# Odd mixer of a two-layer block: depthwise-convolution taps shared out anew between two engines, and the layer norm's sums moved in TensorE's order

## The chip, the cores and the metric

One core of a Trainium2 chip runs the kernel. The metric is the device time of one execution in microseconds (us), in fp32 throughout. TensorE (PE) multiplies matrices into PSUM, VectorE (DVE) and ScalarE (ACT) work on SBUF and PSUM, GpSimd (POOL) on SBUF, and SyncE (SP) issues the transfers.

## The reference, cut to what matters

The input is 512 tokens of 1024 channels. It goes through a first block, then a second block of two layers. The last layer is the odd mixer, and the change lies in it alone:

```python
def odd_mixer(h, w_in, dw_w, dw_b, ln_g, ln_b, w_out):
    proj = h @ w_in                                   # 1024 -> 3 x 1024
    a, b, gate = jnp.split(proj, [CONV_WIDTH, 2 * CONV_WIDTH], axis=-1)
    glu = a * jax.nn.sigmoid(b)
    conv = lax.conv_general_dilated(                  # causal, depthwise, 31 taps
        glu, dw_w.astype(glu.dtype), window_strides=(1,), padding=[(CONV_K - 1, 0)],
        dimension_numbers=('NWC', 'WIO', 'NWC'), feature_group_count=CONV_WIDTH)
    cf = conv.astype(jnp.float32) + dw_b.astype(jnp.float32)
    mu = jnp.mean(cf, axis=-1, keepdims=True)         # over the 1024 channels
    var = jnp.mean(jnp.square(cf - mu), axis=-1, keepdims=True)
    cn = (cf - mu) * lax.rsqrt(var + EPS) * ln_g.astype(jnp.float32) + ln_b.astype(jnp.float32)
    y = jax.nn.silu(cn).astype(h.dtype) * jax.nn.silu(gate)
    return y @ w_out
```

## The kernel before, in words

Channels lie on partitions, tokens along the free axis, so the mixer's 1024 channels are eight tiles (m = 0 to 7) of 128 x 512. A large product is made of "units": one unit gives one tile of 128 output channels as 24 matmuls, since each fp32 operand is split into a high and a low part and three products are summed (`mm3`, L302 to L304). The 512 KB of weights for each unit come by one transfer from SP (`prefetch`, L270) into one of three raw buffers, and ScalarE and GpSimd split them. Units have two PSUM banks in turn; a bank is free for the next unit but one when its result has been read.

The mixer's work is written out by hand as the string `P7_ORDER` (L69), and the loop at L1478 emits it step by step:

- a (`glu_tile`): two units, b and a, then the sigmoid on ScalarE and the product on VectorE. GpSimd also builds the small diagonal weights of the tile's taps (`wds`).
- t, u, v (`stack_tile`, L1360): TensorE regroups the product so that four shifts of 32 channels stand on 128 partitions.
- c (`conv_tile`): the 31 taps. A group of four taps is four matmuls of 32 output partitions side by side (L1376), each with two records in the trace; `PE_TAPS` says how many groups a tile has. Three taps (`N_POOL`) are scaled on ScalarE and added on GpSimd. The rest are VectorE's, one multiply-add each: two lead taps onto an SBUF tile (`P7_LEAD`), the others onto the PSUM bank into which TensorE summed its taps, the last from there into the tile `f`. They are not issued at once but kept in a list (`pend`) that is emitted while the next units are (`tick`), and emptied up to a tile by `drain`.
- s (`stats_tile`): the tile's parts are added up, less the mean of tile 0, and the running sum `msum` and the running sum of squares `ssum` are brought on; on GpSimd, but on VectorE for the last tile.
- g (`gate_tile`): one unit and a Silu on ScalarE out of its bank.
- x (`p8_residual`): four transposes of the residual for one block of tokens (L1471), evicted by ScalarE.
- l (`norm_stats`): TensorE sums `msum` and `ssum` over the channels by a matmul with ones (L405, one for each); VectorE makes mean and reciprocal root from them.
- b, n (`norm_tile`): the scale and shift are spread over the tile, then each tile is normalised, put through a Silu, multiplied by its gate and split into high and low parts for the output projection.

TensorE and SP run in the order in which the program emits (`manual_schedule`), VectorE too until l; from l on VectorE is ordered by the scheduler, as ScalarE and GpSimd are throughout. Each engine still runs its own queue in order. After the string comes the output projection: 8 tiles by 4 blocks of tokens, the first two blocks together, tile by tile, into four banks (two of them those of the units), then the third, then the fourth (`p8_last`).

Of the kernel before, what the change touches and what calls it, by code (L numbers as in the profile page):

```python
# [20 lines left out]
C = 128  # L21
# [39 lines left out]
N_FIRST = 6  # L61
N_POOL = (3, 3, 3, 3, 3, 3, 3, 3)
P7_LEAD = 2
PE_TAPS = (4, 4, 4, 4, 4, 4, 4, 4)
N_PE = max(PE_TAPS)
P7_ENG = {mybir.EngineType.PE, mybir.EngineType.SP}
P1_ENG = {mybir.EngineType.PE, mybir.EngineType.SP}
P7_ENG2 = {mybir.EngineType.DVE}
P7_ORDER = 'a0 a1 t0 g0 u0 a2 v1 c0 a3 v2 c1 s0 a4 v3 c2 s1 a5 v4 c3 s2 a6 v5 c4 s3 a7 v6 c5 s4 g1 v7 c6 s5 g2 c7 g3 s6 x0 g4 x1 s7 g5 x2 l0 g6 b0 n0 n1 n2 n3 n4 n5 g7 n6 n7 x3'  # L69
N_W = 10  # L70
RATE = 4.0
P7_LO = (1, 1)
# [80 lines left out]
def build(tc, xT, par, cst, rope, w_ab, w_in, w_rv, w_out, w_up, w_down, a_w, ab_w, c_w, co_w, post1, poolw, out, dbg=None):  # L153
# [8 lines left out]
    act, dve, pe, gps = nc.scalar, nc.vector, nc.tensor, nc.gpsimd  # L162

    def A(out, in_, func=AF.Copy, **k):
        return act.activation(out=out, in_=in_, func=func, **k)  # L165

    def TT(out, in0, in1, o, e=None):
        return (e or dve).tensor_tensor(out=out, in0=in0, in1=in1, op=o)  # L168

    def STT(out, in0, scalar, in1, o0, o1, e=None):  # L170
        return (e or dve).scalar_tensor_tensor(out=out, in0=in0, scalar=scalar, in1=in1, op0=o0, op1=o1)  # L171
# [5 lines left out]
    MUL, ADD, SUB, MAX = ALU.mult, ALU.add, ALU.subtract, ALU.max  # L177


    class Heap:  # L180
# [6 lines left out]
        def fr(self, *ts):  # L187
            self.free.extend(ts)

    def sbuf_heap(n, name, dt=F32, w=T):  # L190
        return Heap([hp.tile([128, w], dt, name=f"{name}{i}") for i in range(n)])

    al = sbuf_heap(N_ACT - 8, "act")
# [20 lines left out]
    fr = al.fr  # L214
# [8 lines left out]
    def cc(name, i=0, n=None):  # L223
        o, w = C_OFF[name]
        n = w if n is None else n
        o += i * n
        if o < C_KEEP:
            return ck[:, o:o + n]
        o -= C_KEEP
        assert o // T == (o + n - 1) // T  # L230
        return cs[o // T][:, o % T:o % T + n]

    def pc(name, i=0, n=1):
        o, _ = P_OFF[name]
        return pr[:, o + i * n:o + (i + 1) * n]
# [3 lines left out]
    def bc4(ap, n=NCH):  # L239
        return ap.unsqueeze(1).to_broadcast([ap.shape[0], n, ap.shape[1]])  # L240
# [40 lines left out]
    def take():  # L281
        return made.popleft()
# [31 lines left out]
    def tick(n=RATE):  # L314

        credit[0] += n
        while pend and credit[0] >= 1:
            credit[0] -= 1
            pend.popleft()[1]()
        if not pend:  # L320
            credit[0] = min(credit[0], 0)

    def drain(m):
        while pend and pend[0][0] <= m:
            credit[0] -= 1
            pend.popleft()[1]()
# [162 lines left out]
    n0 = P_OFF["attn_w"][1]  # L489
# [517 lines left out]
    acc = []  # L1007
    for t, p in enumerate(units(2 * KF, X, outer=4)):
# [5 lines left out]
        if gu:  # L1014
# [8 lines left out]
            acc = []  # L1023
# [15 lines left out]
    for (k0, kn) in SEGS:  # L1039
        for m in range(KD):  # L1040
            w = take()
# [40 lines left out]
    v2 = lambda t: t.rearrange("p (e n) -> p e n", e=2)  # L1082
# [59 lines left out]
    for g in range(4):  # L1142
# [10 lines left out]
        w = POOL_W[g]  # L1153
# [3 lines left out]
        p = pm()  # L1157
# [30 lines left out]
    for v in stv:  # L1188
        i = next(i for i, t in enumerate(al.free) if t is v)
# [145 lines left out]
    cf, wds = [], {}  # L1335
# [3 lines left out]
    def glu_tile(m):  # L1339

        drain(m - 3)
        nb = 4 * PE_TAPS[m]
        wds[m] = al()
        TT(wds[m][:, :nb * 32].rearrange("p (b c) -> p b c", c=32), bc4(cc("eye"), nb),
           pc("dwp", m, 4 * N_PE)[:, :nb].unsqueeze(2).to_broadcast([128, nb, 32]), MUL, e=gps)
        sg = al()
        A(sg, next(src), AF.Sigmoid)
        TT(gp[m % len(gp)][:, PAD:], next(src), sg, MUL)
        credit[0] -= 1
        fr(sg)  # L1350
# [14 lines left out]
    def conv_tile(m):  # L1365


        g, st = gp[m % len(gp)], stk[m % 2]
        tap = lambda s: pc("dww", m * CONV_K + CONV_K - 1 - s)
        sh = lambda s: g[:, PAD - s:PAD - s + T]  # L1370
        n_e = PE_TAPS[m]
        acc = pm()
        for i in range(n_e):
            for q in range(4):
                o = q * TP + LEFT - 4 * i
                pe.matmul(acc[32 * q:32 * q + 32], lhsT=wds[m][:, i * C + 32 * q:i * C + 32 * q + 32],  # L1376
                          rhs=st[:, o:o + T], start=i == 0, stop=i == n_e - 1)
        fr(wds[m])
        n_p = N_POOL[m]
        t_p, t_d = range(CONV_K - n_p, CONV_K), list(range(4 * n_e, CONV_K - n_p))  # L1380
        aP = al()
        A(aP, sh(t_p[0]), AF.Identity, scale=tap(t_p[0]), bias=pc("dwb", m))
        aQ = None
        for s in t_p[1:]:
            t = al()
            A(t, sh(s), scale=tap(s))
            if aQ is None:
                aQ = t
            else:
                TT(aQ, aQ, t, ADD, e=gps)  # L1390
                fr(t)
        f = al()
        cf.append(f)
        t_a, t_f = t_d[:P7_LEAD], t_d[P7_LEAD:]

        def step(s):
            if s in t_a:
                STT(aP, sh(s), tap(s), aP, MUL, ADD)
            else:
                STT(f if s == t_f[-1] else acc, sh(s), tap(s), acc, MUL, ADD)  # L1400
            if s == t_d[-1]:
                pm.fr(acc)
                if m == 0:
                    TT(aP, aP, aQ, ADD)
                    TT(f, f, aP, ADD)
                    fr(aP, aQ)

        for s in t_d:
            pend.append((m, lambda s=s: step(s)))
        tick(1 + 1.3 * n_e)  # L1410
        return aP, aQ
# [65 lines left out]
    aP, xt = [None] * KD, [None] * NCH  # L1477
    for step in P7_ORDER.split():  # L1478
        o, m = step[0], int(step[1])
        if o == "a":  # L1480
            glu_tile(m)
            if m == 0:
                fr(*yp)
                dump("x2", res)
        elif o in "tuv":
            stack_tile(m, {"t": (0, 1), "u": (2, 3), "v": range(4)}[o])
        elif o == "c":
            aP[m] = conv_tile(m)
            if m >= KD - 2:
                al.fr(*stv[4 * (m % 2):4 * (m % 2) + 4])  # L1490
            if m == KD - 1:
                lent[1] = 0
        elif o == "s":
            stats_tile(m, *aP[m])
        elif o == "g":
            gate_tile()
        elif o == "l":
            order.close()
            order.enter_context(tc.manual_schedule(engines=P7_ENG))
            norm_stats()  # L1500
        elif o == "x":
            xt[m] = p8_residual(m)
        elif o == "b":
            spread(rbc, lr)
            spread(m0, lb)
        else:
            norm_tile(m)
# [74 lines left out]
def _tiles(w, cols):  # L1582

    k = w.shape[0] // 128
    w = w[:, cols] if cols is not None else w
    n = w.shape[1] // 128
    return np.ascontiguousarray(w.reshape(k, 128, n, 128).transpose(2, 1, 0, 3)).reshape(n, 128, k * 128)
# [7 lines left out]
def _arrays(inp):  # L1595
# [7 lines left out]
    for step in P1_ORDER.split():  # L1603
# [14 lines left out]
    W["c_w"] = _tiles(g["c_w_in_2"][0], np.concatenate(  # L1618
        [t(o + int(s[1]) * 128) for s in P7_ORDER.split() if s[0] in "ag" for o in ((1024, 0) if s[0] == "a" else (2048,))]))
    W["co_w"] = g["c_w_out_2"][0].reshape(8, 128, D)  # L1620
# [57 lines left out]
```

## Time and profile before

| what | us |
|---|---|
| median of 3 runs | 1139.08 (1135.81, 1139.08, 1139.31) |
| the profiled execution, its own time | 1135.39 |
| its span | 1133.6 |
| TensorE busy in the span | 1094.7 |
| VectorE, ScalarE, GpSimd busy | 766.1, 523.9, 269.7 |

The span is from the first to the last instruction of the profiled execution; its own time has 1.8 us around the span. Busy times of one engine are unions of its instructions. The stage that the change is in lies at about 920 to 1133 us of the span.

### The profile page before, as it was taken

Reading aid. Unit: us, or ns where it says so; the run is one execution under the profiler, and the core shown is the slowest. Engines: PE = TensorE matmul, PEld = TensorE weight load, DVE = VectorE, ACT = ScalarE, POOL = GpSimd, SP = SyncE. Lnnn points to the kernel's source line nnn. Section 1 sums busy time; section 2 is a strip of 40 time slices with the busy share of each in tenths; the row PEclk is TensorE's granted clock in tenths of the full one; section 3 lists DMA queues with packets and bytes.
Section 4 is the critical chain, followed back from the end, with each engine's and each line's share of the span. In section 5 each row is a group of like instructions: output and inputs, shape, how many; then the busy total and the mean of one; then the engine's idle time right before and its main releaser. Section 6 shows DMA issues by size and latency. Waiting matters only on the chain.

```text
span 1133.6 us, 17775 instructions
## 1 busy us (share of the span) xinstructions
PE 1094.7 (97%) x6848; PEld 881.1 (78%) x6848; DVE 766.1 (68%) x1550; ACT 523.9 (46%) x1044; POOL 269.7 (24%) x242
## 2 busy tenths in 40 slices
PE   8989999999999999999999999999997899999987
PEld 5768787888888888888888888777897886665766
DVE  7978567577568877666733254679758846669785
ACT  6774353225434544444533263555444474454351
POOL 0562231101120000000000052000005464989350
PEclk9989999999999999999999999999998899999989
DMA  7331212113233222333333332211233222221111
GB/s 277 116 93 40 59 57 75 57 47 127 88 101 104 94 93 93 101 104 93 93 100 96 98 112 75 75 38 56 93 112 94 75 89 79 75 58 55 41 53 75
DMA packets 29525, 98.12 MB, mean 87 GB/s; under 512 B 3616, under 2 KB 3872, under 8 KB 29440
## 3 DMA queue, kind: packets, MB, share of 16 engines
q1 hardware_dynamic: 28512, 93.97, 26.4%
q0 software_dynamic: 928, 3.02, 0.8%
q8 instruction: 54, 0.88, 0.3%
q14 instruction: 31, 0.25, 0.1%
HBM read 94.87 MB, written 2.10 MB: 86 GB/s over the span
## 4 chain that ended last, share of the span: by engine, by line
PE 83%; DVE 10%; ACT 4%; issue 1%; DMA 1%; SPq 0%; DVEq 0%; ACTq 0%
PE bank L302 24%; PE bank L303 23%; PE bank L304 23%; DVE act L168 3%; PE bank L1376 3%; DVE act L171 1%; PE bank L1127 1%; PE bank L1092 1%; ACT act L165 1%; ACT op L165 1%; PE bank L704 1%; PE bank L1360 1%; DVE stk L171 1%; ACT whi L165 1%; ACT L165 1%
## 5 line engine op out<-in xcount | busy, mean ns | idle before, releaser
L302 PE MATMUL bank<-op,whi 128*128 128x512 f32 (+1 forms) x568 | 219.2, 386 | 3.3 <-DVE rnt L168 3.3
L302 PE MATMUL bank<-op,op 128*128 128x512 f32 (+1 forms) x561 | 214.9, 383 | 4.5 <-ACT op L165 3.5
L304 PE MATMUL bank<-op,wlo 128*128 128x512 f32 (+1 forms) x565 | 214.4, 379 | 0.0
L303 PE MATMUL bank<-op,whi 128*128 128x512 f32 (+1 forms) x564 | 213.4, 378 | 0.0
L304 PE MATMUL bank<-op,op 128*128 128x512 f32 (+1 forms) x564 | 212.5, 377 | 0.0
L303 PE MATMUL bank<-op,op 128*128 128x512 f32 (+1 forms) x557 | 210.5, 378 | 1.4 <-DVE op L168 1.4
L165 ACT ACTIVATE op<-raw 128x512 fp32r<-128x512 f32 (+1 forms) x166 | 102.8, 625 | 178.7 <-PE bank L303 164.1
L165 ACT ACTIVATE whi<-raw 128x512 fp32r<-128x512 f32 (+1 forms) x168 | 103.3, 622 | 170.3 <-PE bank L303 149.3
L302 PEld LDWEIGHTS bank<-op,whi 128*128 128x128 f32 x568 | 108.4, 191 | 23.5 <-issue 4.5
L302 PEld LDWEIGHTS bank<-op,op 128*128 128x128 f32 x561 | 106.5, 190 | 24.0 <-ACT op L165 3.7
L304 PEld LDWEIGHTS bank<-op,op 128*128 128x128 f32 x564 | 106.9, 190 | 21.0 <-issue 1.7
L304 PEld LDWEIGHTS bank<-op,wlo 128*128 128x128 f32 x565 | 107.5, 190 | 20.1 <-issue 0.5
L303 PEld LDWEIGHTS bank<-op,whi 128*128 128x128 f32 x564 | 107.4, 190 | 19.1 <-issue 1.1
L303 PEld LDWEIGHTS bank<-op,op 128*128 128x128 f32 x557 | 105.7, 190 | 21.1 <-DVE op L168 2.0
L168 POOL TENSOR_TENSOR act<-act,act 128x512 f32<-128x512 f32 x57 | 79.6, 1402 | 87.1 <-ACT act L165 80.3
L168 DVE TENSOR_TENSOR op<-raw,op 128x512 fp32r<-128x512 f32 (+1 forms) x91 | 62.3, 688 | 38.6 <-ACT op L165 37.9
L165 ACT ACTIVATE act<-act 128x512 f32<-128x512 f32 (+3 forms) x123 | 58.3, 479 | 54.1 <-DVE act L168 23.7
L168 DVE TENSOR_TENSOR wlo<-raw,whi 128x512 fp32r<-128x512 f32 (+1 forms) x94 | 63.4, 678 | 25.6 <-ACT whi L165 25.4
L168 POOL TENSOR_TENSOR wlo<-raw,whi 128x512 fp32r<-128x512 f32 x45 | 59.0, 1321 | 79.3 <-ACT whi L165 76.4
L168 DVE TENSOR_TENSOR act<-act,act 128x256 f32<-128x256 f32 (+2 forms) x103 | 70.3, 716 | 6.0 <-ACT act L165 4.4
L168 POOL TENSOR_TENSOR op<-raw,op 128x512 fp32r<-128x512 f32 x44 | 59.5, 1359 | 48.1 <-ACT op L165 41.3
L168 DVE TENSOR_TENSOR bank<-bank,act 128x512 f32<-128x512 f32 x56 | 38.6, 695 | 47.0 <-PE bank L304 47.0
(384 smaller groups left out, 1813.6 us busy)
## 6 DMA issues: line engine op xcount, KB each, us to landing
raw<-in_w_up_dram SPq DMA_DIRECT2D x44, 512.0 KB, 3.5
raw<-in_w_in_dram SPq DMA_DIRECT2D x25, 512.0 KB, 3.5
raw<-in_c_w_dram SPq DMA_DIRECT2D x24, 512.0 KB, 3.5
raw<-in_a_w_dram SPq DMA_DIRECT2D x18, 512.0 KB, 3.5
raw<-in_w_down_dram SPq DMA_DIRECT2D x16, 448.0 KB, 3.3
raw<-in_ab_w_dram SPq DMA_DIRECT2D x12, 512.0 KB, 3.5
raw<-in_w_out_dram SPq DMA_DIRECT2D x8, 512.0 KB, 3.6
raw<-in_w_down_dram SPq DMA_DIRECT2D x8, 512.0 KB, 3.4
```

The source lines that it names most:

```text
L165: return act.activation(out=out, in_=in_, func=func, **k)
L168: return (e or dve).tensor_tensor(out=out, in0=in0, in1=in1, op=o)
L171: return (e or dve).scalar_tensor_tensor(out=out, in0=in0, scalar=scalar, in1=in1, op0=o0, op1=o1)
L302: pe.matmul(ps, lhsT=l[0], rhs=r[0], start=first, stop=False)
L303: pe.matmul(ps, lhsT=l[0], rhs=r[1], start=False, stop=False)
L304: pe.matmul(ps, lhsT=l[1], rhs=r[0], start=False, stop=last)
L704: pe.matmul(p[pt(i), c * c32:(c + 1) * c32], lhsT=l[pt(i), c * c32:(c + 1) * c32], rhs=r[pt(i), c * c32:(c + 1) * c32], start=True, stop=True)
L1092: pe.matmul(v2(psc[e])[:, i, lo:], lhsT=qT[sl, ch(b)], rhs=kT[sl, (b - 1) * C + lo:(b + 1) * C], start=True, stop=True)
L1127: pe.matmul(po[64 * e:64 * e + 64, ch(b)], lhsT=vtok[:, kb * C + 64 * e:kb * C + 64 * e + 64], rhs=v2(pT)[:, i, ch(j)], start=j == 0 or b ...
L1360: pe.matmul(pq[32 * j:32 * j + 32], lhsT=cc("eye")[sl], rhs=g[sl, LEFT + j:LEFT + j + T], start=True, stop=True)
L1376: pe.matmul(acc[32 * q:32 * q + 32], lhsT=wds[m][:, i * C + 32 * q:i * C + 32 * q + 32], rhs=st[:, o:o + T], start=i == 0, stop=i == n_e - 1)
```

## The change

`PE_TAPS` goes from four groups for each tile to three for tiles 0 to 5, four for tile 6 and six for tile 7. VectorE's taps follow from it: sixteen, twelve and four of them, where each tile had twelve. A tile with more than four groups has its diagonal weights in two buffers. The parameter table has room for six groups for each tile, so it grows by 64 columns. In the order, the sums of tile 7 (s7) and the norm's statistics (l0) stand behind the first transposes (x0) and ahead of g4, x1, g5 and x2; before, s7 stood behind x1 and l0 behind x2.

```diff
-PE_TAPS = (4, 4, 4, 4, 4, 4, 4, 4)
+PE_TAPS = (3, 3, 3, 3, 3, 3, 4, 6)
 N_PE = max(PE_TAPS)
...
-P7_ORDER = 'a0 a1 t0 g0 u0 a2 v1 c0 a3 v2 c1 s0 a4 v3 c2 s1 a5 v4 c3 s2 a6 v5 c4 s3 a7 v6 c5 s4 g1 v7 c6 s5 g2 c7 g3 s6 x0 g4 x1 s7 g5 x2 l0 g6 b0 n0 n1 n2 n3 n4 n5 g7 n6 n7 x3'
+P7_ORDER = 'a0 a1 t0 g0 u0 a2 v1 c0 a3 v2 c1 s0 a4 v3 c2 s1 a5 v4 c3 s2 a6 v5 c4 s3 a7 v6 c5 s4 g1 v7 c6 s5 g2 c7 g3 s6 x0 s7 l0 g4 x1 g5 x2 g6 b0 n0 n1 n2 n3 n4 n5 g7 n6 n7 x3'
...
         drain(m - 3)
-        nb = 4 * PE_TAPS[m]
-        wds[m] = al()
-        TT(wds[m][:, :nb * 32].rearrange("p (b c) -> p b c", c=32), bc4(cc("eye"), nb),
-           pc("dwp", m, 4 * N_PE)[:, :nb].unsqueeze(2).to_broadcast([128, nb, 32]), MUL, e=gps)
+        wds[m] = []
+        for i in range(0, PE_TAPS[m], 4):
+            nb = 4 * min(4, PE_TAPS[m] - i)
+            w = al()
+            TT(w[:, :nb * 32].rearrange("p (b c) -> p b c", c=32), bc4(cc("eye"), nb),
+               pc("dwp", m, 4 * N_PE)[:, 4 * i:4 * i + nb].unsqueeze(2).to_broadcast([128, nb, 32]), MUL, e=gps)
+            wds[m].append(w)
...
-                pe.matmul(acc[32 * q:32 * q + 32], lhsT=wds[m][:, i * C + 32 * q:i * C + 32 * q + 32],
+                pe.matmul(acc[32 * q:32 * q + 32], lhsT=wds[m][i // 4][:, i % 4 * C + 32 * q:i % 4 * C + 32 * q + 32],
                           rhs=st[:, o:o + T], start=i == 0, stop=i == n_e - 1)
-        fr(wds[m])
+        fr(*wds[m])
```

## Rows read from the trace of the kernel before

**Rows 1.** The page: busy time of each engine; GB/s in 40 slices.

```profile
PE 1094.7 (97%) x6848; PEld 881.1 (78%) x6848; DVE 766.1 (68%) x1550; ACT 523.9 (46%) x1044; POOL 269.7 (24%) x242
...
GB/s 277 116 93 40 59 57 75 57 47 127 88 101 104 94 93 93 101 104 93 93 100 96 98 112 75 75 38 56 93 112 94 75 89 79 75 58 55 41 53 75
```

**Rows 2.** Windows: stretch, us, busy PE, PEld, DVE, ACT, POOL; PEclk, DMA, GB/s.

```profile
1004.00:1020.00 16.00, 16.00 (x144) 10.21 (x112) 10.79 (x15) 7.52 (x13) 14.80 (x12) 1.00 0.26 69
...
1063.00:1084.00 21.00, 16.87 (x67) 12.39 (x66) 19.91 (x35) 10.42 (x18) 10.48 (x8) 0.88 0.25 75
```

**Rows 3.** Chain that ended last, 1003 to 1063: start, us, what.

```profile
1003.49 1.07 PE bank L1360 x32
...
1019.26 1.07 PE bank L1360 x32
1020.33 3.59 PE bank L1376 x32
...
1049.15 0.88 PE bank L1471 x8
...
1062.71 0.88 PE bank L405 x2
```

**Rows 4.** Timeline, VectorE, 1019 to 1064: start, us, what, idle before.

```profile
1019.35 0.69 DVE L168 TENSOR_TENSOR gp<-bank,act 128x512 f32<-128x512 f32 x1 [3.21 <-PE bank L304]
1019.96 2.44 DVE L171 SCALAR_TENSOR_TENSOR act<-gp,pr,act 128x512 f32<-128x512 f32 x2
1023.97 7.09 DVE L171 SCALAR_TENSOR_TENSOR bank<-gp,pr,bank 128x512 f32<-128x512 f32 x9 [1.57 <-PE bank L1376]
...
1042.28 3.14 DVE L171 SCALAR_TENSOR_TENSOR stk<-gp,pr,stk 128x512 f32<-128x512 f32 x2
...
1053.31 1.42 DVE L168 TENSOR_TENSOR stk<-stk 128x512 f32<-128x512 f32 x2
1054.83 1.36 DVE L168 TENSOR_TENSOR act<-act,stk 128x512 f32<-128x512 f32 x2
1063.61 0.72 DVE L411 STREAM_TRANSPOSE act<-bank 128x512 f32<-128x512 f32 x1 [7.42 <-PE bank L405]
```

**Rows 5.** Timeline, TensorE, 1079 to 1084: the output projection's begin.

```profile
1079.72 0.80 PE L302 MATMUL bank<-op,op 128*128 128x512 f32 x1 [3.49 <-ACT op L165]
...
1083.15 0.79 PE L302 MATMUL bank<-whi,op 128*128 128x512 f32 x1 [0.64 <-ACT stk L165]
```

**Rows 6.** Windows around stretches of the lower clock and one without.

```profile
1079.10:1086.00 6.90, 5.64 (x12) 3.60 (x13) 6.90 (x9) 5.49 (x10) 3.26 (x2) 0.51 0.25 77
...
68.80:72.20 3.40, 3.40 (x10) 2.66 (x9) 1.09 (x7) 3.37 (x11) 2.37 (x2) 0.50 0.46 154
...
936.00:942.00 6.00, 6.00 (x64) 3.42 (x66) 2.30 (x2) 3.83 (x8) 3.83 (x3) 1.00 0.52 134
```

**Rows 7.** Chain that ended last, TensorE's last matmul.

```profile
1127.35 0.13 PE bank L304
```

**Rows 8.** Timeline, GpSimd, 1031 to 1050: sums of tiles 5 and 6.

```profile
1031.99 6.06 POOL L168 TENSOR_TENSOR act<-act,act 128x512 f32<-128x512 f32 x4 [0.60 <-DVE act L171]
...
1043.13 6.06 POOL L168 TENSOR_TENSOR act<-act,act 128x512 f32<-128x512 f32 x4
```

**Rows 9.** Groups by form, 920 to 1134: busy us, mean ns, idle before.

```profile
L171 DVE SCALAR_TENSOR_TENSOR bank<-gp,pr,bank 128x512 f32<-128x512 f32 x72 | 54.4, 756 | 10.7 <-PE bank L1376 8.3
...
L168 DVE TENSOR_TENSOR act<-act,act 128x512 f32<-128x512 f32 x17 | 19.4, 1191 | 0.0
...
L168 POOL TENSOR_TENSOR act<-ck,pr 128x512 f32<-128x512 f32 x4 | 4.5, 1136 | 3.0 <-PE bank L1376 2.9
```

**Rows 10.** Timeline, ScalarE: the eviction with the last gate's Silu.

```profile
1082.53 0.57 ACT L165 ACTIVATE stk<-bank 128x512 f32<-128x512 f32 x1
```

**Rows 11.** Timeline, TensorE: two short idle times elsewhere in the kernel.

```profile
67.13 1.05 PE L648 MATMUL bank<-ck,act 128*128 128x1 f32 x8 [1.76 <-ACT act L165]
...
933.81 0.50 PE L302 MATMUL bank<-whi,op 128*128 128x512 f32 x1 [1.20 <-ACT act L165]
```

## The prediction

> **What bounds the kernel now.** I read the page first: TensorE is busy for 97% of the span [rows 1], so a change counts only if it takes work from TensorE or closes one of the few places where TensorE stands or runs slowly. The windows by stage then split the odd mixer. In the tile stage (1004 to 1020 us) TensorE is busy for all 16.00 us, VectorE for 10.79, GpSimd for 14.80; in 1063 to 1084 TensorE has only 16.87 of 21.00 us, a granted clock of 0.88, and VectorE is nearly full [rows 2]. So the first stage is TensorE's, and the second belongs to the layer norm's chain on VectorE.
>
> The chain of waits shows the beat of the first stage: transposed stacks (L1360) for one tile start at 1003.49 and for the next at 1019.26, 15.77 us per tile; the 32 records of the taps (L1376) take 3.59 us of it [rows 3]. A tile has four groups, so a group costs 0.90 us. VectorE in one period [rows 4]: the gated product 0.69 us, after 3.21 us idle; two lead taps 2.44; 1.57 idle for TensorE's taps; nine taps in 7.09, which is 0.788 each; one last tap like them. VectorE has 4.8 us of idle per tile.
>
> The end of the stage is where time is lost. VectorE finishes the last tile's sums at 1054.83 + 1.36 = 1056.2 us, then stands for 7.42 us [rows 4], because TensorE's two sums (L405) are in its queue behind units g4 and g5, two transposes (x1, x2), and run at 1062.71 [rows 3]. The norm's chain starts at 1063.61. Behind the sums TensorE has only g6, g7 and x3 to do; it is out of work at 1076.23, stands 3.49 us for the first normalised tile, later 0.64 us for a ScalarE eviction [rows 5], and the clock is at its lower level, 1.2 GHz (0.51 of full in the mean), for 1079.1 to 1086 [rows 6]. From there it runs through to 1127.48 [rows 7].
>
> **The change, part by part.**
>
> Fewer taps on TensorE in tiles 0 to 5: six groups of 0.90 us, 5.4 us less. Two more in tile 7: 1.8 us more. Net 3.6 us off TensorE, all ahead of the sums, and TensorE is the bound there.
>
> More taps on VectorE: four more for tiles 0 to 5, 4 x 0.788 = 3.15 us per tile; eight fewer for tile 7, 6.3 us less. VectorE's period: 0.69 + 2.44 + 14 x 0.788 = 14.2 us of work, against TensorE's new 15.77 - 0.90 = 14.87. The cover is the idle time: the 3.21 us before the product falls to about 0.1, and the wait for the taps to 0.6. Were the cover gone, each us per tile would come out as lateness of the last tile. I cost the added taps at nothing for tiles 0 to 4, with 0.7 us per tile to spare, and walk the end in steps.
>
> The end on VectorE. In the trace tile 5's taps onto PSUM begin when TensorE's taps end at 1023.91 [rows 3, 4]; five shorter tiles and tile 5 itself bring that to 1018.5. Fourteen taps: 1029.5. Tile 6 (unchanged, twelve): 2.44 + 10 x 0.788, 1039.8. Tile 7 has four taps: two leads 3.14 [rows 4], two more 1.6, 1044.5. Then four additions into the sums. They took 1.42 + 1.36 us [rows 4], 0.7 each, with GpSimd idle; now GpSimd is at tile 6's sums beside them. Those begin at 1040.9: tile 5's four additions (6.06 us in [rows 8]) now start at 1029.6, and behind them come four GpSimd operations of about 1.3 us, which fill the time from 1038.0 to 1043.1 in [rows 8]. They end at 1047.0. The price under such company: the additions between SBUF tiles average 1.19 us [rows 9]. I take 1.19 for two, and 0.7 to 1.19 for the other two, of which the last also waits for tile 6's sum: the first sum is ready at about 1047.6 and the second at 1048.5. Bounds: 1047.0 (all at 0.7) and 1051.
>
> On these additions a rule can be weighed. The row gives 1.19 us beside GpSimd. The Trainium skill ("SBUF — State Buffer", Who interferes with whom) says that a VectorE operation with two SBUF inputs and a GpSimd operation that reads SBUF lock each other out, and the loser "fully blocks". By it each addition could wait out a GpSimd addition of some 1.4 us before its own 0.7, the sums would come at about 1051, and the forecast would lose 3 us or more; the mean of the rows is between that and no contention.
>
> TensorE at the sums. x0 ends at 1049.15 + 0.88 = 1050.0 [rows 3]; less 3.6, 1046.4. So TensorE, whose queue holds g4, x1, g5, x2, g6, g7, x3 and the output projection behind L405, stands 1.2 us for the first sum and 0.4 for the second: 1.6 us. L405 itself (0.88) only moves. SP's issues are in the units and keep their order; the sums issue no DMA. ScalarE loses nothing: the square of tile 7 is 0.6 us earlier in its order.
>
> Behind the sums. TensorE now has four units and three transposes: from 1050.0 to 1076.2 less 0.9 of L405, 25.3 us of work. The norm's chain from the sums to the first matmul of the projection takes 1079.72 - 1062.71 = 17.0 us [rows 3, 5], so the first normalised tile is there 8 us before TensorE asks. What goes: the idle 3.49 and 0.64 us, and 5.64 us of matmuls at half clock [rows 6], 2.8 us; together 6.9. What is late next: the evictions of the last gate unit. It ran at 1082.53 [rows 10], some 7 us after its unit, since ScalarE stood in order behind the norm; the projection's second bank is this one, and 0.6 to 1 us of its latency has no cover now. I take 0.7 (bounds 0 and 2).
>
> Small: the weights of the taps on GpSimd (1.14 us for 16 blocks, [rows 9]) are a quarter shorter for six tiles, with one more instruction of half the size for tile 7, far ahead of its use; GpSimd's 14.80 of 16 us leaves room for a period of 14.87. 64 more columns of parameters are 32 KB, 0.1 us at the 277 GB/s of the first slice [rows 1], behind the first loads.
>
> **Sum:** -5.4 + 1.8 + 1.6 - 6.9 + 0.7 = -8.2 us, on the profiled execution's 1135.39: 1127.2. The median of the runs shown is 1139.08, 3.7 above that execution, and one run of three is at 1135.8; against the median the forecast is **1130.9**. A measurement of this kernel can tell about 0.3%, 3.4 us, from no change.
>
> **Rivals.**
>
> *The stall at the sums takes the clock with it* (20%). An idle of 1.76 us was followed by the lower level for 3.4 us; one of 1.20 was not [rows 6, 11]; my 1.6 us is between. Price up to half of 6.9 us, 3.4: 1134.3. For it: the two gaps are close together. Against: TensorE is full on both sides of them.
>
> *The sums are late by the lock* (7%), as above: 1051, a stall of 4.6 us and the lower clock: -8.2 + 3.0 + 3.4 = -1.8, 1137.3.
>
> *ScalarE's order* (7%): its queue puts the last gates behind the norm's Silus as it does now; a wait like the 7 us in [rows 10], of which some 1.6 is covered, and the clock: -8.2 + 5 + 3, about no change, 1139. Against it: the norm is through earlier than the gates this time.
>
> *Slower: VectorE becomes the bound of the tiles* (9%). If the added taps cost not 0.788 but as much as the leads, 1.22 us each, a period is 14.2 + 1.7 = 15.9 us against 14.87, and the lead is lost by about 1 us per tile, and more in tile 5, whose wait is gone: some 8 us at the sums, and the lower clock: -8.2 + 8 + 3.4 = +3.2 or more, 1142 to 1144. It decides where the sums come later than about 1056. For it: 0.7 us per tile is little. Against it: all 72 taps onto PSUM average 0.756 us [rows 9], with GpSimd busy for nine tenths of the time beside them.
>
> **How the numbers follow.** Forecast 57%. Its own bounds (stall 0.4 to 3, eviction 0 to 2) give -10 to -6 us. From the profiled execution's level that begins at 1125.4, from the median's it ends at 1133; the clock's case is at 1134.3, the lock's at 1137.3. A range from 1125.4 to 1137.3 leaves out the order's and VectorE's cases, 16%. Faster by over 0.3%: the forecast and the clock's case, 0.77; within 0.3%: lock and order, 0.14; slower 0.09.
>
> **What would show it.** Right: L1360 at a beat of 14.9 us; 24 records of L1376 in 2.7 us for tiles 0 to 5 and 48 in 5.4 for tile 7; VectorE's wait before the product near zero; L405 at about 1047.6 to 1048.9 with 1 to 2 us of idle; no wait for ScalarE's first normalised tile and a clock of 1.00 from x3 on; the projection's start at about 1075. Wrong: a beat over 15 us with TensorE waiting for VectorE; an idle of 4 us at L405; a lower clock behind it; TensorE standing before g6, g7 or the projection for ScalarE.

## The result, and the profile after

The changed kernel takes 1144.14 us in the median, against 1139.08 for the kernel before in the same rounds: the ratio is 1.0054, with a 95% interval of 1.0031 to 1.0076. Faster by 0.7% was forecast; it is slower by 0.5%. The profiled execution has a span of 1138.7 us, 5.0 more than before.

Three stretches show where the time went. They are cut at marks of TensorE's timeline: its first tap record (940.58 us before, 938.18 after), the end of the first transposes x0, the end of the last transposes x3, and the last instruction.

| us | first tap to end of x0 | to end of x3 | to the last instruction | sum |
|---|---|---|---|---|
| before | 109.44 | 26.20 | 57.39 | 193.0 |
| forecast | 105.8 | 27.8 | 51.2 | 184.8 |
| after | 106.11 | 33.09 | 61.28 | 200.5 |

The sum grew by 7.4 us; the stage merely began 2.4 us earlier in this execution, ahead of the taps and of all that is reordered (over the profiled executions of this study its begin lies between 938.2 and 946.1), which leaves 5.0.

TensorE's timeline of the changed kernel has three rows with long idle times behind the tiles:

```profile
1048.41 3.78 PE L405 MATMUL bank<-act,ck 128*128 128x512 f32 x4 [4.11 <-DVE act L168]
...
1080.21 0.50 PE L302 MATMUL bank<-op,op 128*128 128x512 f32 x1 [2.82 <-ACT stk L165]
1087.18 0.80 PE L302 MATMUL bank<-whi,op 128*128 128x512 f32 x1 [5.93 <-ACT stk L165]
```

The first is the wait for the sums, which did not exist before: there L405 follows the transposes at once [rows 3]. The other two stand where [rows 5] had 3.49 and 0.64 us, but both now wait for ScalarE's evictions, not for a normalised tile. The clock fell to its lower level, 0.50 of full, at both places. These are windows of the changed kernel around them (columns as in [rows 2]), with a full one behind:

```profile
1046.80:1053.60 6.80, 5.19 (x8) 2.84 (x9) 4.31 (x10) 0.84 (x2) 1.00 (x1) 0.50 0.00 1
1077.40:1091.20 13.80, 5.07 (x13) 3.64 (x14) 9.40 (x7) 9.29 (x18) 11.42 (x9) 0.63 0.17 59
1091.20:1130.00 38.80, 38.80 (x186) 32.69 (x185) 12.38 (x43) 7.61 (x20) 3.11 (x3) 1.00 0.16 54
```

**The tiles.** VectorE's timeline, against [rows 4]:

```profile
1012.91 0.69 DVE L168 TENSOR_TENSOR gp<-bank,act 128x512 f32<-128x512 f32 x1
1013.51 2.97 DVE L171 SCALAR_TENSOR_TENSOR act<-gp,pr,act 128x512 f32<-128x512 f32 x2
1016.50 10.26 DVE L171 SCALAR_TENSOR_TENSOR bank<-gp,pr,bank 128x512 f32<-128x512 f32 x13
...
1042.45 3.01 DVE L168 TENSOR_TENSOR act<-act,stk 128x512 f32<-128x512 f32 x2
1046.61 1.74 DVE L168 TENSOR_TENSOR act<-act,act 128x512 f32<-128x512 f32 x1 [1.15 <-POOL act L168]
1048.27 0.68 DVE L168 TENSOR_TENSOR act<-act,stk 128x512 f32<-128x512 f32 x1
```

Thirteen taps take 10.26 us, 0.789 each, the price of before. The 3.21 us ahead of the product are gone, and TensorE never waits for VectorE in the tiles. A window over all the tiles' taps (columns as in [rows 2]) has TensorE busy throughout and VectorE for 99.83 of 104.82 us:

```profile
938.18:1043.00 104.82, 104.82 (x740) 66.71 (x730) 99.83 (x120) 48.91 (x85) 85.24 (x65) 1.00 0.21 65
```

But the last additions, 0.7 us each in [rows 4], take 1.5, 1.5 and 1.74, with a wait for GpSimd between. GpSimd's timeline says why (tile 6's sums are the row at 1041.94):

```profile
1027.13 3.00 POOL L168 TENSOR_TENSOR op<-raw,op 128x512 fp32r<-128x512 f32 x2
1030.10 5.71 POOL L168 TENSOR_TENSOR act<-act,act 128x512 f32<-128x512 f32 x4
...
1038.49 1.78 POOL L168 TENSOR_TENSOR wlo<-raw,whi 128x512 fp32r<-128x512 f32 x1
1040.24 1.74 POOL L168 TENSOR_TENSOR op<-raw,op 128x512 fp32r<-128x512 f32 x1
1041.94 5.86 POOL L168 TENSOR_TENSOR act<-act,act 128x512 f32<-128x512 f32 x4
...
1069.51 5.81 POOL L168 TENSOR_TENSOR wlo<-raw,whi 128x512 fp32r<-128x512 f32 x1 [3.73 <-ACT whi L165]
```

Tile 6 is ready for its sums at 1037.72 + 0.75 = 1038.5 us (VectorE's last tap of it), but two weight splits stand ahead in GpSimd's queue and are themselves slowed; the sums run from 1041.94 to 1047.80, just beside VectorE's. In the last row one split takes 5.81 us instead of 1.3, in a stretch where VectorE runs two-input operations back to back; the shift of a norm tile (1075.28, two operations in 2.52 us) stands behind it.

**ScalarE behind the sums** (timeline):

```profile
1076.60 0.82 ACT L165 ACTIVATE act<-act,pr 128x512 f32<-128x512 f32 x1 [3.97 <-POOL act L168]
...
1079.58 0.57 ACT L165 ACTIVATE stk<-bank 128x512 f32<-128x512 f32 x1
...
1083.42 0.63 ACT L165 ACTIVATE op<-act 128x512 fp32r<-128x512 f32 x1 [2.04 <-DVE act L168]
...
1086.55 1.55 ACT L165 ACTIVATE stk<-bank 128x512 f32<-128x512 f32 x3
```

The Silu of g6 runs at 1079.58 and that of g7 is the first of three at 1086.55. TensorE starts 0.06 us behind the end of each. Its units had ended at about 1070.9 and 1076.5. In between ScalarE stood for a norm tile that GpSimd had not shifted (3.97) and for one on VectorE (2.04). Before, the Silu of g6 ran ahead of all Silus of the norm. ScalarE's timeline of the kernel before, with the Silu of g6 and the norm's first:

```profile
1070.27 0.58 ACT L165 ACTIVATE stk<-bank 128x512 f32<-128x512 f32 x1
...
1072.28 0.82 ACT L165 ACTIVATE act<-act,pr 128x512 f32<-128x512 f32 x1 [0.92 <-DVE act L168]
```

Before, none of the norm's eight Silus is ahead of g6's in ScalarE's timeline and four are ahead of g7's; in the changed kernel it is seven and eight.

### The profile page after: what moved, and what is told of

Its sections match the earlier page's. It is cut to its first block, busy times and chain, and to the rows that moved or that the text cites. A ratio compares the mean times of both kernels' runs of the same rounds, so it can differ in the third digit from the quotient of the medians.

```text
span 1138.7 us, 17727 instructions
## 1 busy us (share of the span) xinstructions
PE 1092.4 (96%) x6816; PEld 879.5 (77%) x6816; DVE 778.0 (68%) x1566; ACT 522.5 (46%) x1044; POOL 272.8 (24%) x243
## 4 chain that ended last, share of the span: by engine, by line
PE 71%; DVE 18%; ACT 4%; issue 3%; POOL 2%; DMA 1%; SPq 0%; DVEq 0%; POOLq 0%; ACTq 0%
PE bank L302 21%; PE bank L303 20%; PE bank L304 20%; DVE bank L171 5%; DVE act L168 3%; DVE act L171 3%; PE bank L1127 1%; PE bank L1092 1%; ACT act L165 1%; ACT op L165 1%; PE bank L704 1%; ACT whi L165 1%; POOL act L168 1%; ACT stk L165 1%; POOL wlo L168 1%
## 5 line engine op out<-in xcount | busy, mean ns | idle before, releaser
L168 POOL TENSOR_TENSOR wlo<-raw,whi 128x512 fp32r<-128x512 f32 x45 | 64.1, 1435 | 75.9 <-ACT whi L165 73.3
```

## The experiments

Each kernel is timed against the kernel before, in rounds of its own. In all expectations, theory A is the sums' wait with its clock, B the gates' Silus late in ScalarE's queue, C the taps themselves.

**e1: the taps alone.** The new `PE_TAPS` and weights, with the old order:

```diff
-... s6 x0 s7 l0 g4 x1 g5 x2 g6 b0 ...
+... s6 x0 g4 x1 s7 g5 x2 l0 g6 b0 ...
```

> The new sharing of the taps with the old order. Theory A (TensorE stands at the sums because they are asked for too early, and the clock falls with it) and theory B (the early norm puts the last gates' Silus late in ScalarE's queue) both expect: the beat of the tiles 14.87 us as in the changed kernel, no idle before L405, the projection's wait as in the kernel before (3.5 us and 0.6), so 3 to 3.5 us faster than before, about 0.997. Theory C (the added VectorE taps themselves cost the time) expects it slower than before, by some 5 us.

Measured: 1134.21 us, ratio 0.9959 (0.9938 to 0.998). The stretches are 106.25, 26.20 and 58.96 us, and the waits at the projection are those of before, to the hundredth (TensorE's timeline of e1):

```profile
1082.02 0.80 PE L302 MATMUL bank<-op,op 128*128 128x512 f32 x1 [3.49 <-ACT op L165]
1085.45 0.80 PE L302 MATMUL bank<-whi,op 128*128 128x512 f32 x1 [0.64 <-ACT stk L165]
```

The taps are a gain of 0.4%, and theory C is out. The last stretch of this profiled execution is nonetheless 1.6 us longer than before. The lower clock held until about 1091.3, 5.8 us behind the start of the second of these rows, where before it ended 2.9 us behind it (at 1086, [rows 6]). A window of e1 (columns as in [rows 2]):

```profile
1088.30:1091.70 3.40, 3.40 (x10) 2.66 (x9) 0.00 (x0) 0.13 (x1) 3.24 (x3) 0.52 0.11 16
```

Why it held longer at the same waits is not shown.

**e2: the order alone.** The edit of `P7_ORDER` without that of `PE_TAPS`.

> The old taps (four groups each) with the new order. VectorE's sums come at about 1056 us as before, TensorE is at L405 at 1050. Theory A: an idle of about 6.5 us at L405 and a window of the lower clock (3.4 us), less the 6.9 us that the projection's wait cost: about 3 us slower than before. Theory B: besides that two waits for ScalarE at the projection as in the changed kernel, 8 to 9 us with a lower clock: 10 us or more slower than before. Theory C: same as before.

Measured: 1150.24 us, ratio 1.0096 (1.0078 to 1.0115). TensorE's timeline of e2:

```profile
1058.23 3.41 PE L405 MATMUL bank<-act,ck 128*128 128x512 f32 x4 [5.51 <-DVE act L168]
...
1089.59 0.80 PE L302 MATMUL bank<-op,op 128*128 128x512 f32 x1 [3.46 <-ACT stk L165]
1096.55 0.80 PE L302 MATMUL bank<-whi,op 128*128 128x512 f32 x1 [5.31 <-ACT stk L165]
```

Both waits come with the order, as A and B together said. The new taps soften only the first.

**e3: the sums one unit later.**

```diff
-... s6 x0 s7 l0 g4 x1 g5 x2 g6 b0 ...
+... s6 x0 s7 g4 x1 l0 g5 x2 g6 b0 ...
```

> As the changed kernel, but with l0 behind g4 and x1 (s7 stays behind x0), so that TensorE has 6.3 us of work while the last sums are made. Theory A: idle before L405 under 0.5 us, clock 1.00 there, 7 to 9 us faster than the changed kernel, so about 3 us faster than before. Theory B: the idle at the sums goes but the two waits for ScalarE at the projection stay or grow (8 to 12 us with the lower clock), so only 0 to 5 us faster than the changed kernel.

Measured: 1139.17 us, ratio 1.0 (0.9984 to 1.0016); stretches 106.24, 26.16, 62.52. The wait at the sums and its lower clock are gone: the middle stretch is that of before. The end is worse by 1.2 us than in the changed kernel (TensorE's timeline of e3):

```profile
1072.78 0.50 PE L302 MATMUL bank<-op,op 128*128 128x512 f32 x1 [0.71 <-ACT stk L165]
1082.20 0.79 PE L302 MATMUL bank<-whi,op 128*128 128x512 f32 x1 [8.46 <-ACT stk L165]
```

Against the changed kernel that is 5 us less (1139.17 to 1144.14, each beside its own runs of before), where A expected 7 to 9 and B 0 to 5: the part that A named is gained, and the part that B named stays.

**e4: the last gate earlier in the program**, for theory B: `... g6 g7 b0 n0 ... n7 x3`.

> As the changed kernel, but with g7 written ahead of b0 and the norm tiles, so that the last gate's Silu has its place before the norm's Silus in the scheduler's order; TensorE's order is the same. Theory B: the waits of TensorE for ScalarE at the projection (2.8 and 5.9 us) fall to 0 to 2 us in sum and the clock stays up there: 8 to 11 us faster than the changed kernel, 3 to 6 us faster than before. Theory A: the 4.1 us at L405 stay, and the waits at the projection stay too, since they come from the norm's lateness: same as the changed kernel.

Measured: 1144.24 us, ratio 1.0044 (1.0027 to 1.0061), waits of 4.05, 3.33 and 5.31 us. A miss, and no test of B either: in ScalarE's timeline the Silus of g6 and g7 run at 1080.95 and 1087.91, still behind seven and eight of the norm's. Here an earlier place in the program did not change their place in ScalarE's queue, which the scheduler makes.

**e5: no GpSimd in the norm**, on top of e3:

```diff
-        TT(cf[m], cf[m], lbc, ADD, e=gps if m % 2 else dve)
+        TT(cf[m], cf[m], lbc, ADD)
```

> As e3 (l0 behind g4 and x1), but the norm's shift of the odd tiles is added on VectorE too, so that no Silu of the norm waits for GpSimd. Theory G (ScalarE's queue stands for GpSimd, whose shift of a tile is queued behind a weight split that VectorE's additions lock out for 4 us): ScalarE's wait of 3.5 us for GpSimd goes, the last gates' Silus come 3 to 4 us earlier, TensorE's 9.2 us at the projection fall to 5 or 6, some 4 us faster than e3. Theory S (the place of the last gates in ScalarE's queue, behind norm tiles that wait for VectorE, is what counts): VectorE has four more additions, the wait stays at 8 to 10 us, same time as e3 within 2 us.

Measured: 1129.31 us, ratio 0.9923 (0.9906 to 0.9939); last stretch 53.02 us, 9.5 less than in e3. Rows of TensorE's, GpSimd's and VectorE's timelines of e5, the last two on either side of a long idle time:

```profile
1078.90 0.49 PE L302 MATMUL bank<-whi,op 128*128 128x512 f32 x1 [2.67 <-ACT stk L165]
...
1069.29 13.13 POOL L168 TENSOR_TENSOR wlo<-raw,whi 128x512 fp32r<-128x512 f32 x1 [4.82 <-ACT whi L165]
...
1062.66 6.57 DVE L168 TENSOR_TENSOR act<-act,act 128x512 f32<-128x512 f32 x9
...
1080.60 0.68 DVE L168 TENSOR_TENSOR act<-act,act 128x512 f32<-128x512 f32 x1
1088.33 0.90 DVE L168 TENSOR_TENSOR op<-act,op 128x512 fp32r<-128x512 f32 x1 [7.05 <-ACT op L165]
```

The direction is G's, the size is double: besides ScalarE's wait, the norm's first nine two-input operations on VectorE run in 6.57 us where e3 needs 9.86, and with 2.67 us of idle the clock stays up. The place in the queue, theory S, is not the cause: in e3 and in e5 alike the Silus of g6 and g7 stand behind four and six of the norm's. The price is a GpSimd split of 13.13 us, for which TensorE does not wait here.

**e6: other banks for the projection**, on top of e3, so that TensorE needs no Silu of a gate to begin:

```diff
-    pu.fr(pm(), pm())
+    pu.free.extendleft([pm() for _ in range(4)])
...
-    p8_last(3, [pm(), pm(), pu()], xt[3])
+    p8_last(3, [pu(), pu(), pu()], xt[3])
```

> As e3, but the first four banks of the output projection are those of the transposes and the row sums, none of them the two units' banks that the Silus of g6 and g7 must empty. Theory B (TensorE waits for these Silus and for nothing else): the 0.7 and 8.5 us of idle go, the clock stays 1.00 over the projection's begin, and the projection starts at the end of x3; what then comes last is the split of the last weights, up to 3 us: 7 to 12 us faster than e3 and than before. Theory N (the normalised tiles themselves are too late, the banks are only what shows): the idle turns into waits for ScalarE's or VectorE's parts of the normalised tiles and the time is that of e3 within 2 us.

Measured: 1133.41 us, ratio 0.9953 (0.9936 to 0.9969); last stretch 55.51, 7.0 less than in e3. No idle is left at the projection's begin, and the next thing late is a weight split on GpSimd (TensorE's timeline of e6):

```profile
1090.21 0.50 PE L303 MATMUL bank<-op,whi 128*128 128x512 f32 x1 [3.58 <-POOL op L168]
```

The normalised tiles were there in time; the banks were what TensorE stood for at the begin. The gain, 5 to 6 us against before and e3, is under the 7 to 12 expected: the split's wait is 3.58 us, and the clock fell behind it.

**e7: the same banks in the changed kernel itself.**

> The changed kernel with the same other banks for the projection; the sums stay directly behind x0. Theory B: the idle of 2.8 and 5.9 us and the lower clock behind it go, 9 to 13 us faster than the changed kernel; the 4.1 us at the sums and the lower clock there stay, so it is 2 to 6 us slower than e6 and 4 to 8 faster than before. Theory N: same as the changed kernel.

Measured: 1135.44 us, ratio 0.9974 (0.9958 to 0.9989); stretches 106.24, 32.16, 53.47. The end loses 7.8 us, the middle keeps its wait (TensorE's timeline of e7):

```profile
1053.65 3.34 PE L405 MATMUL bank<-act,ck 128*128 128x512 f32 x4 [4.02 <-DVE act L168]
...
1096.76 0.50 PE L303 MATMUL bank<-op,whi 128*128 128x512 f32 x1 [3.15 <-POOL op L168]
```

With the banks alone changed, the kernel is 0.3% faster than before instead of 0.5% slower, 8.7 us less than the changed kernel where 9 to 13 were expected, and 3.15 us now go to the split. Theory N is out.

**e8: tile 6's sums on VectorE too**, in the changed kernel, to see the additions without GpSimd beside them:

```diff
-        last = dve if m == KD - 1 else gps
+        last = dve if m >= KD - 2 else gps
```

> The changed kernel, but tile 6's four additions into the sums are VectorE's too, so that GpSimd is not at additions while VectorE makes the last sums. Theory L (VectorE's additions and GpSimd's lock each other out, and the last of VectorE's waits for GpSimd's): each of VectorE's eight additions takes 0.7 us (5.6 in sum) instead of 1.5 to 1.75, no wait for GpSimd, and L405 begins at 3 us behind x0 or less instead of 4.1. Theory M (the additions take their 1.5 us whatever GpSimd does): four more of them, L405 some 5 us later than in the changed kernel, and it is slower by about as much.

Measured: 1144.42 us, ratio 1.0059 (1.0043 to 1.0076). Rows of VectorE's, then of TensorE's timeline of e8:

```profile
1048.73 2.86 DVE L168 TENSOR_TENSOR act<-act,act 128x512 f32<-128x512 f32 x4
1051.51 1.41 DVE L168 TENSOR_TENSOR act<-act,stk 128x512 f32<-128x512 f32 x2
1052.95 0.69 DVE L168 TENSOR_TENSOR act<-act,act 128x512 f32<-128x512 f32 x1
...
1053.69 1.13 PE L405 MATMUL bank<-act,ck 128*128 128x512 f32 x2 [2.86 <-DVE act L168]
1056.20 2.08 PE L405 MATMUL bank<-act,ck 128*128 128x512 f32 x2 [1.38 <-DVE act L168]
```

Each addition takes 0.7 us again, no wait for GpSimd is left, and the first sum comes 2.86 us behind x0 instead of 4.11, as L said. The time did not fall: VectorE's last addition now came behind its first step of the norm (the row at 1052.95 is the seventh of eight), so the second sum waits another 1.38 us, and the waits for ScalarE at the projection are still 2.44 and 5.71 us.

**e11: the changed kernel with e5's edit alone.**

> The changed kernel with this one edit: all shifts of the norm on VectorE. Theory G (GpSimd, locked out by VectorE, holds up ScalarE's queue and with it the last gates' Silus): ScalarE's wait of 4 us for GpSimd goes, TensorE's 2.8 and 5.9 us at the projection fall to 1 to 4 in sum and the lower clock there goes, 6 to 10 us faster than the changed kernel; the 4.1 us and the lower clock at the sums stay, so it is 4 to 8 us slower than e5. Theory S (the place in the queue alone): within 2 us of the changed kernel.

Measured: 1141.17 us, ratio 1.0028 (1.0011 to 1.0046), so about 3 us better than the changed kernel, within the intervals, where theory G said 6 to 10 us: a miss. Rows of ScalarE's and TensorE's timelines of e11:

```profile
1085.28 1.15 ACT L165 ACTIVATE whi<-raw 128x512 fp32r<-128x512 f32 x2 [7.41 <-DMA raw<-in_co_w_dram]
...
1089.75 0.80 PE L302 MATMUL bank<-whi,op 128*128 128x512 f32 x1 [8.33 <-ACT stk L165]
```

ScalarE no longer waits for GpSimd's shift, and TensorE's wait for g6's Silu is gone. But ScalarE waits 7.41 us for a weight transfer, and the three evictions with g7's Silu stand behind it, at 1089.12. A split of 13.13 us on GpSimd is again in the trace; that it held the raw buffer which the transfer needed fits the three buffers, and is argued, not tried by itself. In e5 the same Silu stands ahead of such a wait in the queue.

**e10: e5 and e6 together.**

> e5 and e6 together: l0 behind g4 and x1, all shifts of the norm on VectorE, and other banks for the projection. In e5 TensorE still stood 2.7 us for the last gate's Silu. Theory B expects this idle to go, and what is left to be set by the last weights' split on GpSimd, which was done at 1095.8 in e5 and would be asked for at about 1094: a wait of 1 to 2 us, so 1 to 2.5 us faster than e5. Theory N (the banks only cover another lateness): same as e5 within 1 us.

Measured: 1127.31 us, ratio 0.991 (0.989 to 0.993); stretches 106.11, 26.16, 52.37. The idle for the gate is gone; 1.50 us for a split on GpSimd remain (TensorE's timeline of e10):

```profile
1084.80 0.50 PE L303 MATMUL bank<-op,whi 128*128 128x512 f32 x1 [1.50 <-POOL op L168]
```

It has the lowest median of this study, below both kernels that were compared. Its lead over e5 (0.9923) is within the intervals, so by the time alone theory N of this run is not ruled out.

## Why the prediction was wrong

**The taps: right.** Forecast -3.6 us for the tiles, measured -3.33; the beat is 14.93 us, forecast 14.87. The taps onto PSUM cost 0.789 us as taken, and the rival with VectorE as the bound did not happen. VectorE's slack, though, is nearly used up (4.99 us idle in the 104.82 of the tiles).

**The step "tile 6's sums begin at 1040.9, the first sum is ready at about 1047.6": failed.** In the time of the changed trace, 2.4 us earlier, that is 1038.5 and 1045.2. TensorE was at L405 at 1044.29, as forecast (1044.0). GpSimd began tile 6's sums at 1041.94, and L405 began at 1048.41. I had walked GpSimd's queue with the old durations and an order guessed from the old trace. Two splits came ahead of tile 5's sums, which began at 1030.10 and not at 1027.2 (1029.6 less 2.4), and the two splits that I had ahead of tile 6's sums took 1.75 us each and not 1.3. I also took an average price (1.19 us) for additions which, in exactly this place, all had GpSimd against them; e8 shows 0.7 without it, the trace 1.5 to 1.74 with it. The case that I had worked out for the lock gave 1051, less 2.4: 1048.6, which is close to 1048.41 in part by luck. It had about 2.1 us for each addition and no wait; the trace has 1.5 to 1.74 and, besides, 1.15 us of wait for GpSimd's late sum. The Trainium skill ("SBUF — State Buffer", Who interferes with whom) says that a VectorE operation with two SBUF inputs and a GpSimd operation that reads SBUF lock each other out. The runs agree in kind, with 0.7 us for an addition alone (e8) and 1.5 to 1.74 beside GpSimd's.

**The step "TensorE stands 1.6 us", with the clock as a rival at 20%: failed with it.** An idle of 4.11 us, and then the lower clock for 6.8; the middle stretch is 33.09 us, forecast 27.8. That was two of my rivals, the lock (7%) and the clock, and I had given each a chance by itself; with ScalarE's order, below, three came together. The price of the rival with VectorE as the bound, 1142 to 1144, is near the 1144.14 measured, but by coincidence: its sign, a beat over 15 us with TensorE waiting for VectorE, is not in the trace. My range also summed its bounds loosely: a stall of 3 us and an eviction of 2 give -5.5 us and not -6, which does not move the range.

**The step "the evictions of the last gate unit, 0.7 (bounds 0 and 2)": failed most.** The normalised tiles were early, as forecast: e6 and e7 show that nothing else was missing at the projection's begin. But the Silus of g6 and g7 cost 2.82 and 5.93 us and the clock. The last stretch was forecast at 51.2 us and is 61.28; with other banks (e7) it is 53.47, and in e10, with 1.5 us of idle, 52.37. The trace of before showed this ([rows 10]: 7 us between unit and Silu), and I kept it as a rival at 7% because "the norm is through earlier than the gates this time". Here the earlier norm put more norm work ahead of the gates in ScalarE's queue (seven and eight Silus where there were none and four), and work that waits for two other engines.

Together: 0.3 (tiles) + 5.3 + 10.1 make the 15.6 us between -8.2 and +7.4. A gain of the size that was expected can be had: with both waits taken out, the three stretches of e10 sum to 184.6 us, against 184.8 forecast. But e10 asks for the sums one unit later and has other banks and no GpSimd in the norm; that the change alone holds this gain is not shown.

What stays open: why the scheduler puts the last two Silus where it does. e4 shows only that this earlier place in the program did not move them.

## What to carry to other kernels

When a reduction is asked for "as early as possible", what it frees is work for other engines, whose queues are in order: look at every eviction that must go through those queues in the same stretch, and give the next product banks that do not hang on it. Before moving a wait forward, leave one unit of work between the last producer and the waiting matmul; here 6.3 us of it took the middle stretch from 33.09 to 26.16 us and saved 5 in the whole. Price an operation by rows in which its neighbour is busy with the same thing, not by the mean of all, and add up rivals that share a cause.

## What the runs showed of the hardware that was not expected

A GpSimd operation can wait out many of VectorE's operations, not one: a split that takes 1.3 us alone took 5.81 in the changed kernel and 13.13 in e5 and e11, where VectorE's two-input operations ran back to back beside it. In all three it ended 1.14 to 1.16 us behind the end of VectorE's unbroken row (in e5 that row ends at 1080.60 + 0.68 = 1081.28, the split at 1082.42), a little under the 1.3 us that it takes alone. Not every GpSimd operation waits so: earlier in the changed kernel's norm, at 1058.40 to 1064.1, they took 1.67 to 1.74 us each, and nine of VectorE's took 9.86 us. What decides between the two is not shown.

The clock did not fall with every idle. It stayed up behind 2.67 us (e5) and 3.15 us (e7), and fell behind 3.58 us (e6). The length of an idle time is not all that counts: elsewhere in the kernel before, the lower level came behind 1.76 us and eight matmuls with results of 128x1 [rows 6, 11]. Windows behind the idle times of e5, e7 and e6 in turn (columns as in [rows 2]):

```profile
1078.90:1086.00 7.10, 7.10 (x31) 5.89 (x32) 2.38 (x4) 1.62 (x3) 7.10 (x4) 1.00 0.18 53
```

```profile
1096.80:1103.00 6.20, 6.20 (x27) 5.13 (x28) 0.00 (x0) 1.16 (x2) 2.08 (x2) 1.00 0.27 85
```

```profile
1090.80:1094.00 3.20, 3.20 (x9) 2.50 (x8) 1.20 (x2) 2.40 (x5) 1.55 (x2) 0.50 0.47 164
```
